# VectorE's order at the end of a hybrid decoder layer: bank readings ahead of norm chains, and two products moved from GpSimd

## The chip, the cores and the metric

The kernel runs on one core of a Trainium2 chip. A core has a matrix engine (TensorE, PE in the profile), three engines for elementwise work (VectorE or DVE, ScalarE or ACT, GpSimd or POOL), and SyncE (SP), which here only issues DMA transfers. Each engine works through its own list of instructions in order and waits on semaphores for the others. TensorE writes its sums into banks of PSUM; VectorE or ScalarE reads them from there into SBUF. The metric is the device time of one execution in microseconds; the kernel before takes 1017.37 us (median of three runs, 1017.28 to 1017.38).

## The reference

One decoder layer on 512 tokens of 1024 features, in float32. A first norm and a wide projection feed three mixers (dilated attention, causal pooling, a state space scan), whose gated sum is added to x. Then follow the channel mixer and the final norm, and these two are what this change is about:

```python
x = x + merged @ w_o[i]
x = x + conv_ffn(rmsnorm(x, ln2_g[i]), ffn_w_up[i], ffn_conv_w[i], ffn_conv_b[i], ffn_w_down[i])
return rmsnorm(x, final_g)

def rmsnorm(x, g):
    y = x * lax.rsqrt(jnp.mean(x * x, axis=-1, keepdims=True) + NORM_EPS)
    return y * g

def conv_ffn(u, w_up, conv_w, conv_b, w_down):
    h = causal_dwconv(u @ w_up, conv_w, conv_b)
    a, v = h[..., :D_FF], h[..., D_FF:]
    return (jax.nn.silu(a) * v) @ w_down          # D_FF = 2816
```

## The kernel before

**Products.** A float32 product is made of three products of a rounded format: both factors are split into a high part (a cast, on ScalarE) and a low part (the value minus its high part, on VectorE, line 217), and `mm3` adds high times high, high times low and low times high into one bank. So TensorE needs the low part of the weights (`wl`) only for the last third of a product.

**The down projection.** Its 22 blocks of 128 features are taken in groups of 8, 8 and 6. Each group is a two by two block product by seven quarter products instead of eight (Strassen's scheme): the sums and differences of the activations and of the weight quarters are formed beforehand, and each quarter product goes to one or several quarters of the result. The result is held as `X1[tb, h]`: four row blocks tb of 128 tokens, two column halves h of 512. The last group, `last_group`, is the end of the program; its jobs are `two, five, three, one, six, seven, four`. One job is two half products (`i` is 0 and 1), one for each of two row blocks; each has three times three matmuls. `six` completes the right halves of blocks 0 and 1, `seven` the right halves of blocks 2 and 3, and `four` the left halves of blocks 2 and 3. The three share a pair of banks: each job adds to what the bank holds (`more`), so a half product may start only when the bank's last reading is over. A reading is the `tensor_tensor` on VectorE in `job` that adds the bank to `X1[tb, h]` or takes it from it (line 1656 before, 1659 after).

**The final norm** is made block by block behind these readings. `first(tb, h)` is called when the first half of a block is complete: ScalarE sums its squares, and GpSimd multiplies the half by gamma (line 1606 before). `then(tb, h)` is called when the second half is complete. VectorE makes two values of one column per block (lines 1612 and 1613: the sum of squares over 1024 plus epsilon, and its multiple by -0.5); ScalarE sums the squares of the second half and takes the root of the whole (lines 439 and 464). Then comes what is called a chain here, on VectorE: four instructions on one column, which make the factor of each row with a step of refinement (lines 471 to 474), and one that multiplies the second half by factor and gamma (line 478). ScalarE scales the first half, already multiplied by gamma, with the factor (line 479). The last block differs: VectorE multiplies its second half by gamma (line 468) while ScalarE works, and by the factor afterwards (line 483). Each finished half is stored to memory by a DMA of 256 KB, seven on SyncE and the last one on ScalarE.

**What sets the order.** For TensorE, ScalarE, VectorE and GpSimd the order of instructions is that of the Python code as it is run: there is no scheduler. SyncE's transfers are placed by one. Each job runs `prepare()` before its own matmuls: that forms the low part of the weights of the next job and the high part of the one after. `running` holds generators which `step()`, called after each half product, takes further; in the kernel before, the chains of blocks 0 and 1 are put there behind a delay of two steps, and those of blocks 2 and 3 run at once.

**Names in the order's rows.** `x_5525` and `x_5527` are the right halves of blocks 0 and 1, `x_5688` and `x_5694` the right halves of blocks 2 and 3, `x_5529` and `x_5531` the left halves of blocks 2 and 3. `pb` is a bank, `grow` is gamma, `so_` a sum of squares of the first half, `va_` and `vo_` are the two values of one column (96, 99, 102 and 105 for blocks 0 to 3), `xg` is a half on its way to the store.

Of the kernel before, what the change touches and what calls it, by code (L numbers as in the profile page):

```python
# [13 lines left out]
OP = mybir.AluOpType  # L14
# [4 lines left out]
D = 1024  # L19
KD = D // P  # L20
EPS = 1e-6
# [61 lines left out]
def trunk(ctx: ExitStack, tc, out, x, rel_bias, ln1_g, w_in, b_gate, w_a, pool_w, pool_scale, w_b,  # L83
# [3 lines left out]
    act, dve, pool, pe, sp = nc.scalar, nc.vector, nc.gpsimd, nc.tensor, nc.sync  # L87
# [18 lines left out]
    def T(name, dt=F32, shape=(P, S)):  # L106
        return big.tile(list(shape), dt, name=name, tag="t")
# [7 lines left out]
    def small(name, shape, dt=F32):  # L115
        return tiny.tile(list(shape), dt, name=name, tag="tiny")
# [7 lines left out]
    waiting, running = [], []  # L124
# [13 lines left out]
    def flush():  # L138
        todo = second[:]
        second.clear()  # L140
        for f in todo:
            f()
# [6 lines left out]
    def advance(it, phase):  # L149
        for at in it:  # L150
            if at is None or at > phase:
                return at
        running.remove(it)

    def step():
        flush()
        if waiting:
            running.append(iter(waiting.pop(0)))
        now = [(it, 0) for it in running]
        for phase in (0, ROWS, WHOLE, REST):  # L160
            now = [(it, advance(it, phase) if at == phase else at) for it, at in now]

    def after(n, it):
        for _ in range(n):
            yield
        yield from it
# [269 lines left out]
    def squares(eng, src, ss):  # L436
        junk = T("junk")
        if eng is act:
            act.activation(junk, src, AF.Square, accum_out=ss)
        else:  # L440
            dve.scalar_tensor_tensor(junk, src, 1.0, src, OP.mult, OP.mult, accum_out=ss)

    def grow(src):
        g = [T("grow") for _ in range(2)]
        for h in range(2):
            sp.dma_start(g[h], src[h * S:(h + 1) * S].partition_broadcast(P))
        return g
# [11 lines left out]
    def norm_late(t, g, v0, outs, last, h=1, apart=False):  # L459


        ss, v, sq, r, rt = (small(n, [P, 1]) for n in ("ss", "v", "sq", "r", "rt"))
        squares(act, t, ss)
        act.activation(sq, ss, AF.Sqrt, bias=v0, scale=1.0 / D)
        xg = None
        if not apart:
            xg = T("xg")
            dve.tensor_tensor(xg, t, g[h], OP.mult)
        yield xg

        dve.scalar_tensor_tensor(v, ss, -0.5 / D, last, OP.mult, OP.add)
        dve.reciprocal(r, sq)
        dve.scalar_tensor_tensor(rt, r, v, r, OP.mult, OP.mult)
        dve.scalar_tensor_tensor(rt, rt, 1.5, r, OP.add, OP.mult)

        if apart:
            o1, (o0, x0) = outs()
            dve.scalar_tensor_tensor(o1, t, rt, g[h], OP.mult, OP.mult)
            act.mul(o0, x0, rt)
            return  # L480
        (o1, x1), (o0, x0) = outs(xg)
        act.mul(o0, x0, rt)
        dve.tensor_scalar(o1, x1, rt, None, OP.mult)
# [760 lines left out]
    X1 = {}  # L1244
# [10 lines left out]
    COLS = [[cpool.tile([P, 1], F32, name=f"{n}{tb}") for n in ("so", "va", "vo")] for tb in range(4)]  # L1255
# [317 lines left out]
    fin = {}  # L1573

    def last_group():
        n = (KF - KS) // 2
        quarter = lambda two, h: w_down[KS * P:, h * S:(h + 1) * S].rearrange(
            "(k two p) c -> two p k c", two=2, p=P)[two]
        pairs = range(KS // 2, KF // 2)
        W, A, B = {}, [], []  # L1580

        def side(j):
            if j == "A11":
                return [FS[0, p] for p in pairs]
            if j in ("A12", "A22"):
                half = LO if j == "A12" else HI
                return [[t[:, half] for t in ACTS[2 * p + 1]] for p in pairs]
            return [FS[j, p] for p in pairs]

        def load(i, two):  # L1590
            W[i] = ypool.tile([P, 4, S], F32, name="w3", tag="xs")[:, :n, :]
            sp.dma_start(W[i], quarter(two, 1))

        def plus(i, two, h):
            for k in range(n):
                pool.dma_start(W[i][:, k, :], quarter(two, h)[:, k, :], accum_op=OP.add)

        def begin():
            fin["g"] = grow(final_g)
            act.activation(small("sq", [P, 1]), eps, AF.Sqrt)  # L1600

        def first(tb, h):
            half = 1 - h
            ss, xg = COLS[tb][0], T("xg")
            squares(act, X1[tb, half], ss)
            pool.tensor_tensor(xg, X1[tb, half], fin["g"][half], OP.mult)
            fin[tb] = ss, xg

        def then(tb, h):
            ss, xg0 = fin[tb]  # L1610
            _, v0, vh = COLS[tb]
            dve.tensor_scalar(v0, ss, 1.0 / D, EPS, OP.mult, OP.add)
            dve.tensor_scalar(vh, v0, -0.5, None, OP.mult)
            o = {1 - h: xg0}
            if tb < 3:
                o[h] = T("xg")
                it = norm_late(X1[tb, h], fin["g"], v0, lambda: (o[h], (xg0, xg0)), vh, h, True)
                next(it)
            else:
                it = norm_late(X1[tb, h], fin["g"], v0, lambda xg: ((xg, xg), (xg0, xg0)), vh, h)  # L1620
                o[h] = next(it)

            def rest():
                next(it, None)
                for i in (h, 1 - h):
                    (sp if i == h or tb < 3 else act).dma_start(
                        out[tb * P:(tb + 1) * P, i * S:(i + 1) * S], o[i])
                yield

            if tb < 2:  # L1630
                running.append(after(2, rest()))
            else:
                for _ in rest():
                    pass

        def job(j, raw, form, bank, outs, more=False, op=OP.add, behind=None, side_add=False):
            hi, h = outs

            def body(ws):
                wh, wl = ws  # L1640
                if not more:
                    bank[:] = [MM("pb") for _ in range(2)]
                parts = side(j)
                for i in range(2):
                    o = slice(i * P, (i + 1) * P)
                    mm3(bank[i], lambda k: wh[:, k, :], lambda k: wl[:, k, :],
                        lambda k: parts[k][0][:, o], lambda k: parts[k][1][:, o], range(n),
                        flip=True, onto=more)
                    tb = 2 * hi + i
                    t = X1[tb, h]  # L1650
                    if side_add:
                        r = T("r7")
                        act.copy(r, bank[i])
                        pool.dma_start(t, r, accum_op=OP.add)
                    else:
                        dve.tensor_tensor(t, t, bank[i], op)  # L1656
                    if behind:
                        behind(tb, h)
                    step()

            new = Job([raw] if raw is not None else [], n, S, body)
            new.form, new.once = form, True
            if raw is None:
                new.load = lambda: None
            return new

        def total(out, a, b, op=OP.add):
            dve.tensor_tensor(out, a, b, op)
            return out

        def three_read(tb, h):
            if tb == 0:
                total(four.raw, four.raw, W[2])

        two = job("A12", quarter(1, 0), None, B, (0, 0), side_add=True)
        five = job(1, None, lambda: W[0], B, (1, 1), side_add=True)
        three = job(4, None, lambda: W[1], B, (0, 1), more=True, behind=three_read)
        one = job("A11", quarter(0, 0), None, A, (0, 0), behind=lambda tb, h: first(tb, 1))
        six = job(2, None, lambda: W[2], A, (0, 1), more=True, op=OP.subtract, behind=then)
        seven = job(3, None, lambda: W[1], A, (1, 1), more=True, op=OP.subtract,  # L1680
                    behind=lambda tb, h: first(tb, 0))
        four = job("A22", quarter(1, 0), None, A, (1, 0), more=True, behind=then)
        three.then = lambda: plus(1, 0, 1)

        def soon():
            four.load = None
            fetch(four)
            four.load = lambda: None

        six.load = soon  # L1690
        return load, plus, begin, [two, five, three, one, six, seven, four]
# [202 lines left out]
    ss = row_squares(2, small("ss", [P, 4]), 2)  # L1894
# [105 lines left out]
```

## Time and profile before

| | |
|---|---|
| median of three runs | 1017.37 us |
| the profiled execution's own time | 1017.69 us |
| its span, from the first to the last instruction | 1015.9 us |
| TensorE busy | 1001.6 us, 99% |
| VectorE, ScalarE, GpSimd busy | 730.7, 527.8, 163.1 us |
| granted TensorE clock | 0.997 |

A row of the timeline gives the start in microseconds from the start of the span, the duration, the engine, the line of the program, the operation and the names of output and inputs with their shapes; in brackets stands the idle time before it and what ended that. `PEld` is TensorE's loading of the stationary operand. In a row by stretches, each engine has its busy microseconds and, in brackets, its number of instructions; the last three columns are the granted clock, the busy share of the 16 DMA engines and GB/s. Durations of neighbouring VectorE instructions overlap a little in the trace, so that the distance from start to start, not the duration, is what an instruction adds.

### The profile page before, as it was taken

The page shows a single profiled execution, that of the slowest core. Times are in us where ns is not written, and L with a number is a line of the kernel's source. Part 1 is how long each engine was busy: PE and PEld are TensorE (multiplying, and loading weights), DVE is VectorE, ACT ScalarE, POOL GpSimd, SP SyncE. Part 2 cuts the span into 40 slices and gives each one's busy share as a digit, 9 for nine tenths or more (in the row PEclk, how much of TensorE's full clock was granted, in tenths as well). Part 3 has the DMA queues.
Part 4 walks back from the last instruction along what each step waited for, and adds up shares of the span by engine and source line. Part 5 has one row for each costly group of instructions (what it writes and reads, how often), then busy time and mean ns, then how long its engine had stood idle before and what let it go on. Part 6 is the DMA issues. An engine that isn't in the chain of part 4 may idle for free.

```text
span 1015.9 us, 13689 instructions
## 1 busy us (share of the span) xinstructions
PE 1001.6 (99%) x5360; PEld 853.7 (84%) x5360; DVE 730.7 (72%) x931; ACT 527.8 (52%) x895; POOL 163.1 (16%) x144
## 2 busy tenths in 40 slices
PE   8999999999999999999999999999999999999996
PEld 8998878999988888888888887898888888888884
DVE  6564768577767646676879688768778768695887
ACT  5433546554435566878567245554445444443454
POOL 1691000010000000000055501301111100122032
PEclk9999999999999999999999999999999999999998
DMA  8538222155253344552257345432322323342573
GB/s 267 174 102 210 92 76 76 51 156 156 90 182 116 102 120 109 145 136 72 78 155 193 126 136 158 145 125 84 115 93 83 114 93 116 123 114 76 161 180 101
DMA packets 117727, 127.03 MB, mean 125 GB/s; under 512 B 6787, under 2 KB 96454, under 8 KB 117663
## 3 DMA queue, kind: packets, MB, share of 16 engines
q1 hardware_dynamic: 111887, 116.39, 37.0%
q0 software_dynamic: 5184, 8.92, 5.3%
q8 instruction: 42, 0.69, 0.3%
q10 hardware_dynamic: 592, 0.86, 0.2%
q14 instruction: 22, 0.18, 0.1%
HBM read 121.30 MB, written 3.00 MB: 122 GB/s over the span
## 4 chain that ended last, share of the span: by engine, by line
PE 95%; DVE 3%; DMA 1%; issue 1%; ACT 0%; ACTq 0%; DVEq 0%
PE pa L238 36%; PE pu L238 23%; PE pb L238 9%; PE pd L238 7%; PE pqk L238 6%; PE pq L238 3%; PE pa L1848 2%; PE ps L775 1%; PE ppw L238 1%; PE po L823 1%; DVE wl L217 1%; PE pt L809 1%; PE py L1108 1%; PE pu L1536 1%; DMA xin<-in_x_dram 1%
## 5 line engine op out<-in xcount | busy, mean ns | idle before, releaser
L217 DVE TENSOR_TENSOR wl<-raw,wh 128x2048 fp32r<-128x2048 f32 (+3 forms) x86 | 199.5, 2319 | 43.8 <-ACT wh L195 33.9
L195 ACT CAST wh<-raw 128x1024 fp32r<-128x1024 f32 (+3 forms) x169 | 169.9, 1022 | 50.1 <-DVE raw L361 17.8
L1433 DVE SCALAR_TENSOR_TENSOR hc<-pu,fcol,hc 128x510 f32<-128x510 f32 x88 | 65.9, 748 | 52.7 <-ACT hc L1430 51.1
L238 PE MATMUL pa<-uh,wh 128*128 128x512 f32 (+1 forms) x368 | 88.8, 381 | 0.0
L238 PE MATMUL pa<-ul,wh 128*128 128x512 f32 (+1 forms) x368 | 86.8, 375 | 0.0
L238 PE MATMUL pa<-uh,wl 128*128 128x512 f32 (+1 forms) x368 | 86.8, 375 | 0.0
L238 PE MATMUL pu<-uh,wh 128*128 128x512 f32 (+1 forms) x352 | 83.5, 379 | 0.0
L238 PE MATMUL pu<-uh,wl 128*128 128x512 f32 (+1 forms) x352 | 83.5, 379 | 0.0
L238 PE MATMUL pu<-ul,wh 128*128 128x512 f32 (+1 forms) x352 | 83.5, 379 | 0.0
L238 PEld LDWEIGHTS pa<-ul,wh 128*128 128x128 f32 x368 | 66.7, 188 | 12.6
L238 PEld LDWEIGHTS pa<-uh,wl 128*128 128x128 f32 x368 | 66.7, 188 | 12.5
L238 PEld LDWEIGHTS pa<-uh,wh 128*128 128x128 f32 x368 | 65.4, 189 | 11.8
L1438 POOL TENSOR_TENSOR hc<-hc 128x512 f32<-128x512 f32 x22 | 29.9, 1359 | 279.4 <-DVE hc L1433 243.3
L238 PEld LDWEIGHTS pu<-uh,wl 128*128 128x128 f32 x352 | 64.2, 188 | 12.4
L238 PEld LDWEIGHTS pu<-ul,wh 128*128 128x128 f32 x352 | 64.2, 188 | 12.4
L238 PEld LDWEIGHTS pu<-uh,wh 128*128 128x128 f32 x352 | 64.1, 188 | 12.4
L1430 ACT ACTIVATE hc<-pu,fcol,fcol 128x512 f32<-128x512 f32 x40 | 31.2, 779 | 74.7 <-PE pu L238 74.7
L217 DVE TENSOR_TENSOR wl<-w,wh 128x2048 fp32r<-128x2048 f32 (+1 forms) x26 | 54.3, 2087 | 10.3 <-issue 4.6
L195 ACT CAST wh<-w 128x1024 fp32r<-128x1024 f32 (+1 forms) x52 | 47.2, 949 | 10.1 <-DVE x L1656 5.3
L797 ACT ACTIVATE sb<-sb,nmls 128x128 f32<-128x128 f32 (+1 forms) x72 | 30.0, 418 | 31.5 <-DVE nmls L794 20.8
L1091 POOL TENSOR_TENSOR st<-st,dts 128x512 f32<-128x512 f32 x4 | 4.2, 1050 | 225.7 <-ACT st L1099 163.6
L1435 ACT ACTIVATE hc<-hc 128x512 f32<-128x512 f32 x22 | 13.9, 633 | 40.6 <-DVE hc L1433 38.6
(438 smaller groups left out, 1977.0 us busy)
## 6 DMA issues: line engine op xcount, KB each, us to landing
raw<-in_w_in_dram SPq DMA_DIRECT2D x24, 1024.0 KB, 6.0
raw<-in_ffn_w_up_dram SPq DMA_DIRECT2D x22, 1024.0 KB, 5.2
raw<-in_w_in_dram SPq DMA_DIRECT2D x14, 512.0 KB, 5.6
raw<-in_w_in_dram SPq DMA_DIRECT2D x8, 768.0 KB
raw<-in_ffn_w_down_dram SPq DMA_DIRECT2D x6, 1024.0 KB, 5.0
raw<-in_w_b_dram SPq DMA_DIRECT2D x4, 1024.0 KB
al<-ad SPq DMA_DIRECT2D x16, 256.0 KB, 6.6
raw<-in_w_c_dram SPq DMA_DIRECT2D x4, 1024.0 KB, 5.1
```

Of the source, the lines that this page charges most:

```text
L195: (other.tensor_copy if other and i else act.copy)(job.high[:, :, o], job.raw[:, :, o])
L217: (eng or dve).tensor_tensor(l[:, :, o], job.raw[:, :, o], h[:, :, o].bitcast(F32), OP.subtract)
L238: pe.matmul(ps, l, r, start=first and n == 0, stop=last and n == total - 1, skip_group_check=onto)
L775: pe.matmul(pss[i][:, o:o + w * P], q[r, n * P:(n + 1) * P], k[r, kb * P:(kb + w) * P], start=True, stop=True)
L797: act.activation(sb[:, off:off + w * P], sb[:, off:off + w * P], AF.Exp, bias=nm[:, n, h:h + 1], accum_out=ls[:, n, h:h + 1])
L809: pe.transpose(pt[:, o:o + P], sb[:, o:o + P], eye)
L823: pe.matmul(po[DH * hh:DH * hh + DH, n * P:(n + 1) * P], V[g, kb + i][:, (2 * c + hh) * DH:(2 * c + hh + 1) * DH], probs[2 * c + hh, nb][: ...
L1430: act.activation(t, ps, AF.Identity, bias=ff["c1"][:, ff["b"] + m:ff["b"] + m + 1], scale=fw(2, m))
L1433: dve.scalar_tensor_tensor(t[:, sh:], ps[:, :S - sh], fw(k, m), t[:, sh:], OP.mult, OP.add)
L1435: act.activation(t, t, AF.Silu)
L1438: pool.tensor_tensor(a, a, t, OP.mult)
L1848: pe.matmul(first[2 * n + j][:, lo:hi], a[:, k, j * P:(j + 1) * P], b[:, k, lo:hi], start=a is wh and b is uh and k == 0, stop=a is wl and ...
```

## The change

Three things are changed, all in the jobs `six`, `seven` and `four` (numbered 2, 3 and A22):

- A chain runs at a fixed place, given by a table `order`: block 0's behind the second reading of `six`, block 1's behind the second reading of `seven`, and those of blocks 2 and 3 behind the last reading of `four`. Before, the first two were behind the first and second reading of `seven`, and the last two each behind their own reading. `seven.late` lets the table also place `prepare()`, that is the low part of the last weights, behind the first reading of `seven`.
- The products with gamma of the right halves of blocks 2 and 3 are VectorE's, together with the two values of one column (`rows`), between the readings.
- Block 3 is treated as the others: one instruction by factor and gamma (line 478) replaces lines 468 and 483.

```diff
             squares(act, X1[tb, half], ss)
-            pool.tensor_tensor(xg, X1[tb, half], fin["g"][half], OP.mult)
             fin[tb] = ss, xg
+            if tb < 2:
+                pool.tensor_tensor(xg, X1[tb, half], fin["g"][half], OP.mult)
+
+        def rows(tb, h):
+            if tb > 1:
+                dve.tensor_tensor(fin[tb][1], X1[tb, 1 - h], fin["g"][1 - h], OP.mult)
+            ss, v0, vh = COLS[tb]
+            dve.tensor_scalar(v0, ss, 1.0 / D, EPS, OP.mult, OP.add)
+            dve.tensor_scalar(vh, v0, -0.5, None, OP.mult)
 
         def then(tb, h):
             ss, xg0 = fin[tb]
             _, v0, vh = COLS[tb]
-            dve.tensor_scalar(v0, ss, 1.0 / D, EPS, OP.mult, OP.add)
-            dve.tensor_scalar(vh, v0, -0.5, None, OP.mult)
-            o = {1 - h: xg0}
-            if tb < 3:
-                o[h] = T("xg")
-                it = norm_late(X1[tb, h], fin["g"], v0, lambda: (o[h], (xg0, xg0)), vh, h, True)
-                next(it)
-            else:
-                it = norm_late(X1[tb, h], fin["g"], v0, lambda xg: ((xg, xg), (xg0, xg0)), vh, h)
-                o[h] = next(it)
+            if tb < 2:
+                rows(tb, h)
+            o = {1 - h: xg0, h: T("xg")}
+            it = norm_late(X1[tb, h], fin["g"], v0, lambda: (o[h], (xg0, xg0)), vh, h, True)
+            next(it)
...
-            if tb < 2:
-                running.append(after(2, rest()))
-            else:
-                for _ in rest():
-                    pass
+            fin["rest", tb] = rest()
+
+        def end(tb):
+            for _ in fin["rest", tb]:
+                pass
...
                     if behind:
                         behind(tb, h)
+                    for f in order.get((j, i), ()):
+                        f()
                     step()
...
         three.then = lambda: plus(1, 0, 1)
+        seven.late = True
+        order = {(2, 1): [lambda: end(0)],
+                 (3, 0): [lambda: seven.prepare()],
+                 (3, 1): [lambda: rows(2, 0), lambda: end(1)],
+                 ("A22", 0): [lambda: rows(3, 0)],
+                 ("A22", 1): [lambda: end(2), lambda: end(3)]}
```

VectorE before, from behind the second reading of `six` to the second reading of `seven`:

```order
L1612 TENSOR_SCALAR va_99<-so_98 128x1
L1613 TENSOR_SCALAR vo_100<-va_99 128x1
L217 TENSOR_TENSOR wl<-raw,wh 128x1536
L1656 TENSOR_TENSOR x_5688<-x_5688,pb 128x512
L471 SCALAR_TENSOR_TENSOR v<-ss,vo_97 128x1
L472 RECIPROCAL r<-sq 128x1
L473 SCALAR_TENSOR_TENSOR rt<-r,v 128x1
L474 SCALAR_TENSOR_TENSOR rt<-rt,r 128x1
L478 SCALAR_TENSOR_TENSOR xg<-x_5525,rt,grow 128x512
L1656 TENSOR_TENSOR x_5694<-x_5694,pb 128x512
```

The same place after, on to the product with gamma that follows the second reading:

```order
L1614 TENSOR_SCALAR va_99<-so_98 128x1
L1615 TENSOR_SCALAR vo_100<-va_99 128x1
L471 SCALAR_TENSOR_TENSOR v<-ss,vo_97 128x1
L472 RECIPROCAL r<-sq 128x1
L473 SCALAR_TENSOR_TENSOR rt<-r,v 128x1
L474 SCALAR_TENSOR_TENSOR rt<-rt,r 128x1
L478 SCALAR_TENSOR_TENSOR xg<-x_5525,rt,grow 128x512
L1659 TENSOR_TENSOR x_5688<-x_5688,pb 128x512
L217 TENSOR_TENSOR wl<-raw,wh 128x1536
L1659 TENSOR_TENSOR x_5694<-x_5694,pb 128x512
L1612 TENSOR_TENSOR xg<-x_5688,grow 128x512
```

Block 0's chain has moved ahead of the first reading of `seven`, and the low part of the last weights behind it; between the two readings stands the low part alone.

VectorE before, from the first reading of `four` on, with block 2's chain between the two readings:

```order
L1656 TENSOR_TENSOR x_5529<-x_5529,pb 128x512
L1612 TENSOR_SCALAR va_102<-so_101 128x1
L1613 TENSOR_SCALAR vo_103<-va_102 128x1
L471 SCALAR_TENSOR_TENSOR v<-ss,vo_103 128x1
L472 RECIPROCAL r<-sq 128x1
L473 SCALAR_TENSOR_TENSOR rt<-r,v 128x1
L474 SCALAR_TENSOR_TENSOR rt<-rt,r 128x1
L478 SCALAR_TENSOR_TENSOR xg<-x_5529,rt,grow 128x512
L1656 TENSOR_TENSOR x_5531<-x_5531,pb 128x512
```

The same place after:

```order
L1659 TENSOR_TENSOR x_5529<-x_5529,pb 128x512
L1612 TENSOR_TENSOR xg<-x_5694,grow 128x512
L1614 TENSOR_SCALAR va_105<-so_104 128x1
L1615 TENSOR_SCALAR vo_106<-va_105 128x1
L1659 TENSOR_TENSOR x_5531<-x_5531,pb 128x512
L471 SCALAR_TENSOR_TENSOR v<-ss,vo_103 128x1
L472 RECIPROCAL r<-sq 128x1
L473 SCALAR_TENSOR_TENSOR rt<-r,v 128x1
L474 SCALAR_TENSOR_TENSOR rt<-rt,r 128x1
L478 SCALAR_TENSOR_TENSOR xg<-x_5529,rt,grow 128x512
```

Block 2's chain has gone behind the last reading, and block 3's follows it; between the two readings stand a product with gamma and two instructions on one column.

ScalarE before, its last rows:

```order
L439 ACTIVATE junk,ss<-x_5529 128x512
L464 ACTIVATE sq<-ss,va_102 128x1
L479 ACTIVATE xg<-xg,rt 128x512
L439 ACTIVATE junk,ss<-x_5531 128x512
L464 ACTIVATE sq<-ss,va_105 128x1
L482 ACTIVATE xg<-xg,rt 128x512
L1626 DMA out_dram<-xg 128x512
```

And after:

```order
L439 ACTIVATE junk,ss<-x_5529 128x512
L464 ACTIVATE sq<-ss,va_102 128x1
L439 ACTIVATE junk,ss<-x_5531 128x512
L464 ACTIVATE sq<-ss,va_105 128x1
L479 ACTIVATE xg<-xg,rt 128x512 x2
L1629 DMA out_dram<-xg 128x512
```

The scaling of block 2's right half has gone behind the squares and the root of block 3, and stands directly ahead of block 3's scaling. On SyncE the two stores of block 2 keep their order, the half scaled by ScalarE first.

## The prediction

> **What bounds the kernel now.** I read the page first, to see which engine carries the span. The second line gives busy time, share and instruction count of each engine; the third is the chain of work that ended last, by engine.
>
> ```profile
> span 1015.9 us, 13689 instructions
> PE 1001.6 (99%) x5360; PEld 853.7 (84%) x5360; DVE 730.7 (72%) x931; ACT 527.8 (52%) x895; POOL 163.1 (16%) x144
> PE 95%; DVE 3%; DMA 1%; issue 1%; ACT 0%; ACTq 0%; DVEq 0%
> ```
>
> TensorE bounds almost everything, and the change gives it no other work. Only the 3% of the chain that is VectorE's can move, so the second view is the stretches at the end: length, then busy time (and count) of PE, PEld, DVE, ACT, POOL, then clock, DMA share and GB/s.
>
> ```profile
> 998.00:1003.50 5.50, 5.40 (x24) 4.13 (x22) 5.36 (x13) 2.46 (x6) 1.29 (x1) 1.00 0.00 0
> 1003.50:1006.00 2.50, 2.37 (x9) 1.61 (x9) 2.39 (x6) 1.45 (x3) 1.29 (x1) 1.00 0.56 210
> 1006.00:1012.20 6.20, 0.00 (x0) 0.00 (x0) 4.67 (x17) 3.48 (x8) 0.00 (x0) 0.74 0.45 169
> ```
>
> TensorE is done before 1006, and 6 us of VectorE and ScalarE follow. VectorE is full from 998 to 1006: it is late, and stays late. The third view, VectorE's instructions in order of time (start, duration, instruction), says with what.
>
> ```profile
> 997.32 0.69 DVE L1656 TENSOR_TENSOR x<-x,pb 128x512 f32<-128x512 f32 x1 [0.69 <-PE pb L238]
> 997.93 0.15 DVE L1612 TENSOR_SCALAR va<-so 128x1 f32<-128x1 f32 x1
> ...
> 998.18 1.75 DVE L217 TENSOR_TENSOR wl<-raw,wh 128x1536 fp32r<-128x1536 f32 x1
> 999.84 0.68 DVE L1656 TENSOR_TENSOR x<-x,pb 128x512 f32<-128x512 f32 x1
> 1000.44 0.15 DVE L471 SCALAR_TENSOR_TENSOR v<-ss,vo 128x1 f32<-128x1 f32 x1
> ...
> 1000.70 1.21 DVE L473 SCALAR_TENSOR_TENSOR rt<-r,v 128x1 f32<-128x1 f32 x1
> ...
> 1002.81 0.68 DVE L1656 TENSOR_TENSOR x<-x,pb 128x512 f32<-128x512 f32 x1
> ...
> 1007.24 0.16 DVE L471 SCALAR_TENSOR_TENSOR v<-ss,vo 128x1 f32<-128x1 f32 x1 [0.54 <-ACT junk L439]
> ...
> 1007.77 0.22 DVE L473 SCALAR_TENSOR_TENSOR rt<-r,v 128x1 f32<-128x1 f32 x1
> ...
> 1008.22 0.75 DVE L478 SCALAR_TENSOR_TENSOR xg<-x,rt,grow 128x512 f32<-128x512 f32 x1
> 1008.89 0.68 DVE L1656 TENSOR_TENSOR x<-x,pb 128x512 f32<-128x512 f32 x1
> ...
> 1009.74 0.68 DVE L468 TENSOR_TENSOR xg<-x,grow 128x512 f32<-128x512 f32 x1
> ...
> 1011.33 0.49 DVE L483 TENSOR_SCALAR xg<-xg,rt 128x512 f32<-128x512 f32 x1
> ```
>
> One instruction on one column, L473, takes 1.21 us in block 0's chain and 0.22 in block 2's. Rows of ScalarE, TensorE and GpSimd give the reason and the consequence:
>
> ```profile
> 997.35 0.29 ACT L464 ACTIVATE sq<-ss,va 128x1 f32<-128x1 f32 x1
> 998.48 0.84 PE L238 MATMUL pb<-wl,sbh 128*128 128x512 f32 x3
> 1000.61 1.29 POOL L1606 TENSOR_TENSOR xg<-x,grow 128x512 f32<-128x512 f32 x1 [3.67 <-DVE v L471]
> 1003.57 1.29 POOL L1606 TENSOR_TENSOR xg<-x,grow 128x512 f32<-128x512 f32 x1 [1.68 <-DVE v L471]
> 1002.56 0.84 PE L238 MATMUL pb<-wl,fh 128*128 128x512 f32 x3
> 1003.55 0.53 PEld L238 LDWEIGHTS pb<-wh,fh 128*128 128x128 f32 x3 [0.57 <-DVE x L1656]
> 1005.06 0.86 PE L238 MATMUL pb<-wl,fh 128*128 128x512 f32 x3
> ```
>
> GpSimd's product with gamma runs from 1000.61 to 1001.90, and L473, begun at 1000.70, ends at 1001.91; the product at 1003.57 does the same to block 1's chain. So each costs VectorE 1.21 - 0.22 = 0.99 us. For these delays the reading at 1002.81 comes late, the weight loads of TensorE's last half product stand idle 0.57 us for it, and the last bank, full at 1005.06 + 0.86 = 1005.92, is read at 1008.89 only.
>
> **The change part by part.** I rebuild VectorE's sequence from the reading at 997.32, before which nothing is moved. Pitches, start to next start: reading 0.60 (999.84 to 1000.44), low part of the weights 1.66 (998.18 to 999.84), the two one-column rows 0.25 (997.93 to 998.18), a chain with L478 2.37 with the stall (1000.44 to 1002.81), so 1.38 without. A product with gamma on VectorE: L468, the same shape, has 0.68 us, as long as a reading, so 0.60; the upper end would be 1.29, GpSimd's own. I take 0.60, because L468 is the same instruction.
>
> - Chain 0 now stands ahead of the low part: 998.18 to 999.56. Its root was there at 997.35 + 0.29 = 997.64, so order alone held it back.
> - Block 2's reading 999.56 (its bank is full at 998.48 + 0.84 = 999.32), low part 1000.16 to 1001.91. Queued behind the low part is TensorE's last product, which needs it at 1002.56: the 2 us by which it is put back are hidden with 0.65 us to spare, and without that cover each microsecond would be one of TensorE.
> - Block 3's reading 1001.82, done 1002.50. TensorE wants that bank at 1002.56 + 0.68 = 1003.24 (the row is the last of three groups of 0.68) and began at 1003.55: this 0.31 us goes, and it ends near 1005.44. This gain is worth nothing by itself, as VectorE stays later.
> - Product for block 2 at 1002.42, two rows 1003.02, chain 1 1003.27 to 1004.65, reading 1004.65, product for block 3 1005.25, two rows 1005.85, last reading at 1006.10 instead of 1008.89. Nothing waits here for ScalarE: its inputs were made while VectorE was busy.
> - Chain 2 1006.70 to 1008.08, chain 3 until 1009.54. Before, VectorE ended at 1011.33 + 0.49 = 1011.82, so its end comes 2.28 us earlier. By kind: two stalls -1.98, two products +1.20, L468 gone -0.62, L483 of 0.49 replaced by L478 of 0.75 +0.26; the remaining -1.14 is VectorE's idle time ahead of the last two chains, 0.54 of it in the row at 1007.24.
>
> ScalarE's rows of the end show how far its own steps lie after a reading:
>
> ```profile
> 1009.61 0.63 ACT L439 ACTIVATE junk<-x 128x512 f32<-128x512 f32 x1 [0.60 <-DVE x L1656]
> 1010.14 0.18 ACT L439 ACTIVATION_READ_ACCUMULATOR junk<-x 128x1 f32 x1
> 1010.36 0.29 ACT L464 ACTIVATE sq<-ss,va 128x1 f32<-128x1 f32 x1
> ...
> 1011.39 0.72 ACT L482 ACTIVATE xg<-xg,rt 128x512 f32<-128x512 f32 x1 [0.74 <-DVE rt L474]
> 1012.14 0.38 ACTq L1626 DMA_DIRECT2D out_dram<-xg  x1
> ```
>
> Squares start 0.72 after the reading's start, the root ends 1.76 after it: 1006.10 + 1.76 = 1007.86. The scaling of block 2's other half, formerly ahead of block 3's squares, is now behind that root: 1007.8 to 1008.5. Block 3's scaling follows its chain's factor: it starts 0.06 after VectorE's last instruction (1011.39 and 1011.33 before), at 1008.85, and ends at 1009.56. So ScalarE ends 2.5 us earlier, and the last two stores are issued at 1009.56 and 1009.59.
>
> **What is late next: the stores.** SyncE's issue of block 2's two stores, then the DMA traffic of the last two blocks by stretches, then the time from issue to landing of a store:
>
> ```profile
> 1009.03 0.81 SPq L1626 DMA_DIRECT2D out_dram<-xg  x2
> 1009.80:1011.30 1.50, 0.00 (x0) 0.00 (x0) 1.26 (x6) 0.82 (x3) 0.00 (x0) 0.50 0.94 350
> 1011.30:1012.60 1.30, 0.00 (x0) 0.00 (x0) 0.49 (x1) 0.72 (x1) 0.00 (x0) 0.50 0.00 0
> 1012.60:1014.10 1.50, 0.00 (x0) 0.00 (x0) 0.00 (x0) 0.00 (x0) 0.00 (x0) 0.50 0.93 348
> DMA to landing us min/median/max: 2.0/2.0/2.0
> ```
>
> A pair of 256 KB stores fills all 16 DMA engines for 0.94 x 1.50 = 1.41 us, and its traffic begins some 0.83 us after the first issue (issued 1011.83, over at about 1014.07). Before, the pairs of blocks 2 and 3 lie apart, with 1.3 us of nothing between them. Now SyncE, whose list still has the ScalarE half of block 2 first, issues it at 1008.55; the traffic begins at 1009.38, block 3's pair is ready at 1010.4 while 0.4 us of block 2's is left, and the four together need 2 x 1.41 = 2.82: over at 1012.2. The gain is therefore 1014.07 - 1012.2, about 1.88 us, and not 2.28. The 1.8 us from the last byte to the span's end stay.
>
> The Trainium skill, "DMA: Bandwidth & Descriptors", section "Issuing engines are not separate DMA queues", says that issuing from several engines ends on the same 16 DMA engines. By it, the fourth store on ScalarE's queue escapes nothing, which is this sum (1.88); were each queue its own path, it would be 2.28. No run here shows two queues' stores in competition for long.
>
> GpSimd's two products disappear at no cost elsewhere, because nothing else is on its list by then. **Sum:** the profiled execution took 1017.69 us with a span of 1015.9; it becomes 1015.8. The median of the runs is 0.32 lower, 1017.37, and becomes 1015.5, or 0.18% less. About 0.2% (2.03 us) is what a measurement of this kernel can tell from no change, so I forecast a gain just short of it.
>
> **The rivals.**
> - The stores of the last two blocks don't hold each other, because block 2's come a little earlier or transfers overlap better. Then VectorE's 2.28 us arrive whole: 1015.1. For it: the two bounds are only 0.4 us apart. Against it: the DMA share is 0.94 within the stretch, with nothing idle to fill.
> - The stall of L473 isn't GpSimd's doing, and the first two chains still take 2.37 us. Then 1.98 us come back on VectorE and the gain on the stores is 1.88 - 1.98 = -0.1: 1017.5. Against it speak the ends that agree to 0.01 us.
> - Slower: the last store lands late, since four stores of 1 MB in all now reach the memory as one burst. The longest landing in this trace is one of 9.1 us, of the accumulating loads in GpSimd's queue (row below). If the last store took that instead of about 2.6 us (2.0 and the queueing), the end would come 6.5 later: 1022.0. It decides for slower from 3.9 us of extra landing on; against it, the stores that the trace times took 2.0, with two in flight at a DMA share of 0.94.
>
> ```profile
> DMA to landing us min/median/max: 4.1/6.7/9.1
> ```
>
> The Trainium skill, "DMA: Bandwidth & Descriptors", section "Latency and other measured facts", puts the receipt of a write to HBM at 0.2 us on average and 2 us at high load. If the burst were such a load, an estimate by that page is 1.8 us more and 1017.3, no change; the pairs of before, which load the engines as fully, show nothing of it.
>
> **How the numbers follow.** The forecast, stores back to back: 0.60, 1015.5, with 1015.2 to 1015.9 as its own range; the upper end of a product (1.29 for 0.60, twice 0.69) would make it 1016.9. Stores apart: 0.22, 1015.1. The stall stays or the products cost GpSimd's price: 0.12. Late landing: 0.04, and 0.02 for something unforeseen. Of the forecast's 0.60 about 0.13 lie beyond 2.03 us, since a tenth of a microsecond decides. So faster by over 0.2%: 0.22 + 0.13 = 0.35; slower 0.05; within 0.2%: 0.60. The range 1014.9 to 1016.3 takes in the first two cases and half the way to the dearer product.
>
> **What the changed profile would show.** Right: all four L473 near 0.2 us; no GpSimd product after 997; no TensorE wait behind a reading in the last product; the last reading near 1006.1; the four last stores as one stretch of full DMA from 1009.4 to 1012.2; a span near 1014.0. Wrong: if the last product waits for the low part, if there is a gap between the two pairs of stores (then 2.28), or if L473 still reads 1.2.

## The result, and the profile after

| | before | after |
|---|---|---|
| median of 17 runs each | 1017.61 us (1017.04 to 1018.27) | 1015.52 us (1015.09 to 1016.24) |
| profiled execution, and its span | 1017.69, 1015.9 us | 1015.52, 1013.7 us |

The ratio is 0.998, with a 95% interval of 0.9973 to 0.9988: a gain clear of no change, about 2.1 us, and the measurement doesn't tell on which side of 0.2% it lies.

The page's first and third lines after; TensorE's busy time is within 0.5 us of what it was, GpSimd has two instructions less:

```profile
span 1013.7 us, 13681 instructions
...
PE 1001.1 (99%) x5360; PEld 853.4 (84%) x5360; DVE 730.4 (72%) x932; ACT 528.1 (52%) x895; POOL 158.8 (16%) x142
```

VectorE's instructions after, in order of time, at the places shown of before:

```profile
997.35 0.69 DVE L1659 TENSOR_TENSOR x<-x,pb 128x512 f32<-128x512 f32 x1 [0.88 <-PE pb L238]
...
998.47 0.22 DVE L473 SCALAR_TENSOR_TENSOR rt<-r,v 128x1 f32<-128x1 f32 x1
...
999.58 0.68 DVE L1659 TENSOR_TENSOR x<-x,pb 128x512 f32<-128x512 f32 x1
1000.18 1.75 DVE L217 TENSOR_TENSOR wl<-raw,wh 128x1536 fp32r<-128x1536 f32 x1
1001.85 0.68 DVE L1659 TENSOR_TENSOR x<-x,pb 128x512 f32<-128x512 f32 x1
1002.45 0.68 DVE L1612 TENSOR_TENSOR xg<-x,grow 128x512 f32<-128x512 f32 x1
...
1003.56 0.22 DVE L473 SCALAR_TENSOR_TENSOR rt<-r,v 128x1 f32<-128x1 f32 x1
...
1004.67 0.68 DVE L1659 TENSOR_TENSOR x<-x,pb 128x512 f32<-128x512 f32 x1
...
1006.12 0.68 DVE L1659 TENSOR_TENSOR x<-x,pb 128x512 f32<-128x512 f32 x1
...
1008.80 0.75 DVE L478 SCALAR_TENSOR_TENSOR xg<-x,rt,grow 128x512 f32<-128x512 f32 x1
```

L473 has 0.22 us in every chain, no row behind the first waits for another engine, and the last reading starts at 1006.12, where it was 1008.89. VectorE ends at 1009.55 instead of 1011.82.

TensorE's last half product, ScalarE's end and the issue of the last three stores on SyncE, and then the stretches of DMA traffic (columns as before):

```profile
1003.27 0.84 PE L238 MATMUL pb<-wh,fh 128*128 128x512 f32 x3
1007.79 0.71 ACT L479 ACTIVATE xg<-xg,rt 128x512 f32<-128x512 f32 x1
1008.80 0.72 ACT L479 ACTIVATE xg<-xg,rt 128x512 f32<-128x512 f32 x1 [0.31 <-DVE rt L474]
1009.56 0.41 ACTq L1629 DMA_DIRECT2D out_dram<-xg  x1
1008.52 1.39 SPq L1629 DMA_DIRECT2D out_dram<-xg  x3
1009.00:1010.40 1.40, 0.00 (x0) 0.00 (x0) 0.56 (x1) 0.53 (x1) 0.00 (x0) 0.50 0.76 277
1010.40:1012.20 1.80, 0.00 (x0) 0.00 (x0) 0.00 (x0) 0.00 (x0) 0.00 (x0) 0.50 0.98 368
1012.20:1013.60 1.40, 0.00 (x0) 0.00 (x0) 0.00 (x0) 0.00 (x0) 0.00 (x0) 0.50 0.00 0
```

The last half product follows the one before it without a wait (1003.27; before 1003.55). The four stores of blocks 2 and 3, issued on two queues, are one stretch: read in slices of a tenth of a microsecond, the traffic begins at 1009.36 and is over at 1012.14, where before it was over at 1014.11.

### The profile page after: what moved, and what is told of

It reads as the page before. It is cut to its first block, busy times and chain, and to the rows that moved or that the text cites. A ratio compares the mean times of both kernels' runs of the same rounds, so it can differ in the third digit from the quotient of the medians.

```text
span 1013.7 us, 13681 instructions
## 1 busy us (share of the span) xinstructions
PE 1001.1 (99%) x5360; PEld 853.4 (84%) x5360; DVE 730.4 (72%) x932; ACT 528.1 (52%) x895; POOL 158.8 (16%) x142
## 4 chain that ended last, share of the span: by engine, by line
PE 95%; DVE 3%; DMA 1%; issue 0%; ACT 0%; ACTq 0%; DVEq 0%
PE pa L238 36%; PE pu L238 23%; PE pb L238 9%; PE pd L238 8%; PE pqk L238 6%; PE pq L238 3%; PE pa L1859 2%; PE ps L775 1%; PE ppw L238 1%; PE po L823 1%; DVE wl L217 1%; PE pt L809 1%; PE py L1108 1%; PE pu L1536 1%; DMA xin<-in_x_dram 1%; PE pyo L1115 1%
```

## The experiments

The second reading of `six`, ahead of which nothing is moved, starts at 997.3 in the kernel before and anywhere from 997.05 to 997.82 in the executions below. Positions are therefore counted from that reading, and times of whole runs are given only where there are several rounds.

| kernel | L473, chains 0 and 1 | reading to VectorE's end | reading to the end of the traffic | from there to the span's end |
|---|---|---|---|---|
| before | 1.21, 1.21 us | 14.50 us | 16.79 us | 1.79 us |
| after | 0.22, 0.22 | 12.20 | 14.79 | 1.56 |
| order, and block 3 as the others, without the products (e1) | 0.22, 1.14 | 12.47 | 14.87 | 1.38 |
| products alone (e2) | 0.22, 0.22 | 13.96 | 16.21 | 1.76 |
| block 2's scaled half on ScalarE's queue (e4) | 0.22, 0.22 | 12.21 | 14.49 | 1.76 |
| the same, block 3 on SyncE (e10) | 0.22, 0.22 | 12.20 | 14.47 | 1.76 |

(The ends of the traffic are read from how full the last stretches of 0.1 us are, and the profile gives spans to 0.1 us.)

**The order without the products (e1).** Of the three parts of the change, only the products with gamma go back to GpSimd; block 3 is still treated as the others. The theory is the prediction's: GpSimd's products stop VectorE, so both the order and the move of the products are needed. The rival is that GpSimd has nothing to do with L473's 1.21 us.

```diff
-            if tb < 2:
-                pool.tensor_tensor(xg, X1[tb, half], fin["g"][half], OP.mult)
+            pool.tensor_tensor(xg, X1[tb, half], fin["g"][half], OP.mult)
...
-            if tb > 1:
-                dve.tensor_tensor(fin[tb][1], X1[tb, 1 - h], fin["g"][1 - h], OP.mult)
```

> The new order, but the two products with gamma stay on GpSimd (block 2's and block 3's right halves). My theory: GpSimd's products and VectorE's instructions with two operands in SBUF exclude each other, so the products, wherever they fall behind the readings of seven, stop VectorE for about 1 us each, less the 1.2 us that VectorE no longer spends on them. GpSimd's first product is held by the low part of the weights until about 1001.9 and then meets chain 1, the second follows it. I expect at least one L473 (or L471) of about 1 us or more in block 1's chain, the first reading of four near 1005.7 instead of 1004.67, VectorE's end near 1010.3 instead of 1009.55, and a time 0.5 to 1.0 us above the changed kernel's (1016.0 to 1016.5, ratio 0.9985 to before). Rival, the stall isn't GpSimd's doing: no long L471 to L474 here, as in the changed kernel, and VectorE ends 1.2 us earlier, near 1008.4.

The median was 1015.24 us (10 runs), ratio 0.998 (0.997 to 0.9989): as fast as the whole change. VectorE's and GpSimd's rows:

```profile
1002.39 0.40 DVE L471 SCALAR_TENSOR_TENSOR v<-ss,vo 128x1 f32<-128x1 f32 x1
1002.91 1.14 DVE L473 SCALAR_TENSOR_TENSOR rt<-r,v 128x1 f32<-128x1 f32 x1
...
1005.80 0.68 DVE L1656 TENSOR_TENSOR x<-x,pb 128x512 f32<-128x512 f32 x1
...
1006.74 0.16 DVE L472 RECIPROCAL r<-sq 128x1 f32<-128x1 f32 x1 [0.17 <-ACT sq L464]
...
1000.04 3.99 POOL L1607 TENSOR_TENSOR xg<-x,grow 128x512 f32<-128x512 f32 x2 [3.56 <-DVE x L1656]
```

The stall is there, as expected, and the rival falls; but both products fall on one chain, and cost (0.40 - 0.15) + (1.14 - 0.22) = 1.17 us, not 2 times 0.99. GpSimd's first product begins while VectorE makes the low part of the weights and takes 2.74 us instead of 1.29, and its later part lies under a reading and two small rows. The two products on VectorE cost 1.20. So up to the last reading it makes no difference who makes them: that reading starts 8.75 us after the first one here, and 8.77 in the changed kernel. Behind it, block 2's chain waits for ScalarE's root, 0.17 us idle in the row at 1006.74, because block 3's product no longer stands between the last two readings and gives ScalarE time. From L471 to L473 it takes 0.53 us instead of 0.26, and these 0.27 us make up the difference at VectorE's end. At the end of the traffic 0.08 us is left, since SyncE's first issue of the four stores, at 1008.29, comes only 0.07 us later than in the changed kernel, counted from the reading. My expectation of 0.5 to 1.0 us was wrong.

**The products alone (e2).**

```diff
-            pool.tensor_tensor(xg, X1[tb, half], fin["g"][half], OP.mult)
+            (pool if tb < 2 else dve).tensor_tensor(xg, X1[tb, half], fin["g"][half], OP.mult)
```

> The order of before, with the two products on VectorE, behind the readings of seven. My theory: both L473 of 1.21 us become 0.22, the products cost 0.60 each, so the two chains behind them are over 0.77 us earlier; TensorE's wait of 0.3 us before the last half product goes; the idle time of VectorE before the last two chains (1.14 us in all) stays, since their readings still stand right ahead of them. VectorE's end near 1011.05 instead of 1011.82; the pairs of stores of blocks 2 and 3 stay apart, so the end of the stores follows by the same 0.77: 1016.7, ratio 0.9992. Rival, the stall isn't GpSimd's doing: L473 keeps 1.21 us and the end is 1.2 us later than before.

The median was 1017.23 us (11 runs), ratio 0.9996 (0.9987 to 1.0005): not told from no change. Its VectorE rows:

```profile
1000.05 0.68 DVE L1656 TENSOR_TENSOR x<-x,pb 128x512 f32<-128x512 f32 x1
1000.77 0.69 DVE L1606 TENSOR_TENSOR xg<-x,grow 128x512 f32<-128x512 f32 x1
...
1001.63 0.22 DVE L473 SCALAR_TENSOR_TENSOR rt<-r,v 128x1 f32<-128x1 f32 x1
...
1006.92 0.16 DVE L471 SCALAR_TENSOR_TENSOR v<-ss,vo 128x1 f32<-128x1 f32 x1 [0.53 <-ACT junk L439]
```

The stalls are gone, the idle time for ScalarE stays. The gain is 0.54 us at VectorE's end, not 0.77, because a product right behind the reading whose result it uses starts 0.72 us after it and not 0.60; in the changed kernel another block's reading stands between (1001.85 to 1002.45). That is 0.12 us for each of the two. TensorE's matmuls wait only 0.04 us before the last half product (1003.45 to 1003.49), where they waited 0.31 before; that this wait would go was expected.

**GpSimd reading and GpSimd writing (e5, e6).** Is it the reading of SBUF that stops VectorE? Into the changed kernel, behind block 1's product, the first run puts three products that nobody uses, the second eight memsets of the same tile:

```diff
+            if tb == 1:
+                dum = T("dum")
+                for _ in range(3):
+                    pool.tensor_tensor(dum, fin["g"][0], fin["g"][1], OP.mult)
```

```diff
+            if tb == 1:
+                dum = T("dum")
+                for _ in range(8):
+                    pool.memset(dum, 0.0)
```

> The changed kernel with three more products of 128x512 on GpSimd behind its last one (gamma times gamma into a tile that nobody reads), which keep it reading SBUF from about 996.8 to 1000.7 and more, while VectorE does chain 0 (998.2 to 999.6). My theory: VectorE's one-column instructions with two operands in SBUF wait for the GpSimd product in flight, so chain 0 grows from 1.38 us by 1 to 2.5 us, with single instructions of about 1 us in it, and as VectorE never idles from there on, its end and that of the stores come later by as much. Rival, GpSimd has nothing to do with it: chain 0 keeps 1.38 us.

> The same as the run with three products, but with eight memsets of 128x512 on GpSimd, which only write. Theory of the shared way for reads: chain 0 keeps its 1.38 us and the end doesn't move. Rival, any GpSimd work in SBUF stops VectorE: chain 0 grows as with the products.

With products: VectorE's two stopped rows, its low part of the weights, GpSimd's three products, and TensorE's weight load for the last third of the product that needs that low part:

```profile
998.47 0.92 DVE L471 SCALAR_TENSOR_TENSOR v<-ss,vo 128x1 f32<-128x1 f32 x1
...
999.50 1.26 DVE L473 SCALAR_TENSOR_TENSOR rt<-r,v 128x1 f32<-128x1 f32 x1
...
1002.25 1.75 DVE L217 TENSOR_TENSOR wl<-raw,wh 128x1536 fp32r<-128x1536 f32 x1
995.20 5.54 POOL L1612 TENSOR_TENSOR dum<-grow 128x512 f32<-128x512 f32 x3
1004.05 0.53 PEld L238 LDWEIGHTS pb<-wl,fh 128*128 128x128 f32 x3 [0.38 <-DVE wl L217]
```

With memsets:

```profile
998.55 0.22 DVE L473 SCALAR_TENSOR_TENSOR rt<-r,v 128x1 f32<-128x1 f32 x1
996.88 4.62 POOL L1612 MEMSET dum<- 128x512 f32 x8
```

Under 4.62 us of memsets the chain keeps its length; under products it loses 0.77 + 1.04 = 1.81 us, within the 1 to 2.5 us expected. VectorE's end comes 14.01 us after the reading instead of 12.20, which is the same 1.81 us, and the end of the traffic 16.61 instead of 14.79: what stops VectorE in this stretch is paid in full. With memsets VectorE's end is at 12.21. The Trainium skill, "SBUF — State Buffer", section "Who interferes with whom", says that a VectorE instruction with two SBUF inputs contends with a GpSimd instruction that reads SBUF and not with one that only writes; both runs agree, down to VectorE operands of one column.

The run with products also shows that the low part's cover is limited: starting at 1002.25 instead of 1000.18, it makes TensorE wait 0.38 us, though the product had itself begun late. What waits there is the weight load, whose row in the changed kernel is:

```profile
1002.37 0.64 PEld L238 LDWEIGHTS pb<-wl,fh 128*128 128x128 f32 x3
```

Counted to this load the cover is 0.44 us (the low part is done at 1001.93); the prediction's 0.65 counted to the matmul behind it. No run measures the size directly.

**Without block 2's stores (e3).** The changed kernel with the two stores of block 2 left out, so that 128 rows of the output are not written:

```diff
-                for i in (h, 1 - h):
+                for i in (h, 1 - h) if tb != 2 else ():
```

> The changed kernel without the two stores of block 2 (rows 256 to 383 of the output are not written). My theory: block 3's pair then begins its traffic 0.83 us after its first issue at 1009.57 and is over 1.41 us later, near 1011.8 instead of 1012.15: block 2's stores cost 0.35 us. Rival, the stores don't hold each other: the end of the traffic stays at 1012.15.

This execution was late from the start (the reading at 997.82), so the end of the traffic is counted from SyncE's last issue:

```profile
1010.16 0.33 SPq L1629 DMA_DIRECT2D out_dram<-xg  x1
1012.30:1012.40 0.10, 0.00 (x0) 0.00 (x0) 0.00 (x0) 0.00 (x0) 0.00 (x0) 0.50 0.70 246
1012.40:1012.50 0.10, 0.00 (x0) 0.00 (x0) 0.00 (x0) 0.00 (x0) 0.00 (x0) 0.50 0.15 41
```

Over at 1012.42, 2.26 us after the issue. In the changed kernel SyncE's last issue is at 1009.58 and the traffic over at 1012.14, 2.56 us after it (2.54 in its second profile, e8). Block 2's stores hold block 3's by 0.30 us (0.35 expected), and the rival that they don't falls.

**Block 2's first store earlier (e4).**

```diff
-                    (sp if i == h or tb < 3 else act).dma_start(
+                    (sp if i == h or tb < 2 else act).dma_start(
```

> The changed kernel, with the store of block 2's scaled half issued by ScalarE, so that SyncE issues VectorE's half of block 2 first, at 1008.2 instead of 1008.52. My theory: four stores back to back bound the end, from the first one's traffic on, so they are over 0.3 us earlier (near 1011.85 instead of 1012.15), though ScalarE's last scaling starts 0.1 us later for the issue of 0.4 us ahead of it. Rival, the end is that of the last pair alone: no gain, or 0.1 us later, near 1012.2.

SyncE's first issue and ScalarE's two, and the end of the traffic:

```profile
1008.21 0.33 SPq L1629 DMA_DIRECT2D out_dram<-xg  x1
1008.53 0.38 ACTq L1629 DMA_DIRECT2D out_dram<-xg  x1
1009.71 0.35 ACTq L1629 DMA_DIRECT2D out_dram<-xg  x1
1011.80:1011.90 0.10, 0.00 (x0) 0.00 (x0) 0.00 (x0) 0.00 (x0) 0.00 (x0) 0.50 0.37 123
```

The traffic is over at 1011.84, 0.30 us earlier, as expected of four stores in a row: the first issue sets the end of the traffic. The span is only 0.1 shorter, 1013.6, because it ends 1.76 us after the traffic and not 1.56. The median is 1015.45 us (11 runs), ratio 0.9978 (0.9969 to 0.9987): the same as the changed kernel.

**From the traffic's end to the span's end (e7 to e10).** Both kernels were profiled again, to see whether this last figure belongs to the change:

> The kernel before once more, to see in a second profile how far its end repeats: L473 of 1.21 us twice, the last reading near 1008.9, the stores over near 1014.1, and from there 1.8 us to the span's end. If the last figure is as short as the changed kernel's 1.56 us, it isn't the change's doing.

> The changed kernel once more: the last reading near 1006.1, the stores in one stretch from 1009.35 to 1012.15, and from there to the span's end 1.56 us as in its first profile. If it is 1.8 us here, the 0.25 us by which the first profile's span came out shorter than forecast are no part of the change.

Before again: 1.78 us (span 1015.9). After again: 1.66 (span 1013.8). So it is shorter after, by 0.1 to 0.2 us. Then two kernels asked whether ScalarE's queue is the reason:

The kernel before (e9):

```diff
-                    (sp if i == h or tb < 3 else act).dma_start(
+                    sp.dma_start(
```

The changed kernel (e10):

```diff
-                    (sp if i == h or tb < 3 else act).dma_start(
+                    (sp if i == h or tb != 2 else act).dma_start(
```

> The kernel before, with its last store issued by SyncE behind the other half's, instead of by ScalarE. It asks what sets the time from the end of the store traffic to the span's end, 1.78 us in both profiles of before and 1.4 to 1.66 in those of the new order. Theory: the end comes 0.3 us later after the traffic where ScalarE's queue holds the store that was issued last; then it is 1.4 to 1.5 here. Rival: what counts is that block 3's pair stands apart from block 2's; then it stays 1.78. The traffic's end stays as before (near 1014.1) by both.

> The changed kernel with block 2's scaled half stored by ScalarE's queue (as in the run e4) and both halves of block 3 by SyncE's, so that the last store isn't on ScalarE's queue. The traffic of the four stores begins at 1009.05 and is over near 1011.86, as in e4, 0.3 us ahead of the changed kernel's. Theory of the queue that is last: from there 1.4 to 1.5 us to the span's end instead of e4's 1.76, so a span of 1013.3 and a time 0.3 to 0.4 us below the changed kernel's (ratio to before 0.9975). Rival: 1.76 as in e4, a span of 1013.6.

SyncE's issue of the last two stores and the last stretch with traffic, first of before with both on SyncE, then of the changed kernel in that form:

```profile
1011.79 0.81 SPq L1626 DMA_DIRECT2D out_dram<-xg  x2
1014.00:1014.10 0.10, 0.00 (x0) 0.00 (x0) 0.00 (x0) 0.00 (x0) 0.00 (x0) 0.50 0.26 82
```

```profile
1009.60 0.84 SPq L1629 DMA_DIRECT2D out_dram<-xg  x2
1011.80:1011.90 0.10, 0.00 (x0) 0.00 (x0) 0.00 (x0) 0.00 (x0) 0.00 (x0) 0.50 0.42 144
```

With spans of 1015.8 and 1013.6, this leaves 1.77 and 1.76 us: my theory of the last queue falls, and the rival of the pair that stands apart falls too, by e4 and e10. The median of e10 is 1015.28 us (11 runs), ratio 0.9978 (0.9969 to 0.9987). The times don't tell e1, e4 or e10 from the changed kernel.

## Why the prediction was right, point by point

- **The time.** 1015.5 us was forecast and 1015.52 measured, with VectorE's sequence right to 0.03 us (last reading 1006.10 and 1006.12, end 1009.54 and 1009.55), ScalarE's end 1009.56 and 1009.52, the traffic from 1009.38 to 1012.2 and from 1009.36 to 1012.14. TensorE's wait went, and the low part of the weights was done 0.66 us ahead of the matmul that needs it (1001.93 and 1002.59), 0.44 ahead of its weight load. The 2.03 us that the prediction took for the least that can be told was too much: the interval of the ratio is 0.0015 wide, or about 0.8 us to either side.
- **The stores.** That the gain is cut from 2.28 us at VectorE's end to about 1.9 at the stores was right: it is 2.27 and 1.97 by the two traces, and e3 and e4 show the hold of 0.3 us from both sides.
- **A term that was off, and some luck.** "The 1.8 us from the last byte to the span's end stay" was the step that failed: it is 1.56 to 1.66 us. The span is 1013.7 and not 1014.0, and the profiled execution took 1015.52 us and not 1015.8. The step from there to the median failed too: the 0.32 us by which the median of before lay below its profiled execution were 0.08 with 17 runs, and 0.00 after. These two errors cancel in the 1015.5, so the forecast time agrees more closely than its working deserves. The gain was larger than forecast: 2.17 us between the profiled executions and 2.09 between the medians, where 1.88 was forecast.
- **Which part earns it.** The sum was right, but its listing by kind (stalls -1.98, products +1.20) invites a reading that is wrong, and which I held when I wrote what e1 should give: that moving the products is a large part of the gain. Without the products, the change (e1) brings 2.03 of the 2.30 us at VectorE's end and all but 0.08 us at the traffic's end. By rows this is 0.81 of the stalls (1.98 less the 1.17 left) and 0.87 of idle time (1.14 less 0.27); about 0.36 is, by the prediction's sum (-0.62 + 0.26), block 3's treatment, and no run was made with that alone. The products alone bring 0.54 and 0.58, which the time can't show. The stall is no fixed price of a product. It depends on what VectorE has in its list while the product runs: in the old order two chains, in the new one mostly a reading.
- **The rivals.** Stores that don't hold each other: excluded by e3. A stall that isn't GpSimd's: excluded by e2, e5 and e6. Late landing: the traces give no landing time for the store on ScalarE's queue, but the span ends 1.56 to 1.66 us after the traffic, sooner than the 1.78 to 1.79 of before.

## What to carry to other kernels

Where one engine is busy without a gap to the end, write down its list with start-to-start distances from the trace and move it through the new order; here this gave each start to 0.03 us, and the 1.81 us that e5 put into the list came out whole at the end. Put work whose inputs come from another engine behind work that is ready, so that the other engine's time is covered: this earned more here (1.14 us of idle time) than taking the second engine's interference away alone (0.54 us in e2). And look at what stands behind that engine: stores that used to lie apart come to lie in a row when the work before them closes up, and then the first issue, not the last, sets the end of the traffic. Time gained or lost behind that issue counts less: e1's 0.27 us at VectorE's end are 0.08 there.

## What the runs showed that I had not expected

From the last DMA traffic to the span's end it took 1.76 to 1.79 us in before (twice), e2, e4, e9 and e10, and 1.38 to 1.66 in after (twice), e1, e3 and the runs with GpSimd's extra work. In the first group the last two stores were issued 0.12 us or more apart, in the second within 0.05 us of each other and on two queues. Neither the queue of the last store nor the gap to the pair before explains it. That the near simultaneous issue is the cause is only what the two groups suggest; no run was made that changes it alone, and it stays open.
